# First addends of the gate weights' sums moved from GpSimd's transfers to SyncE's queue, in a two-layer encoder trunk

## The chip, the cores and the metric

One core of one Trainium2 chip runs the whole program. The metric is the device time of one execution in microseconds (us); lower is better. The engines are named as in the profile: PE (TensorE's matmuls), PEld (its weight loads), ACT (ScalarE), DVE (VectorE), POOL (GpSimd), SP (SyncE, which here only issues transfers).

## The reference

```python
def reference(x, p, norm_g, na_w_in, na_rpb, na_w_out, mla_w_in, ..., ple_norm, ple_w_gate, ple_w_proj, final_norm):
    for i in range(DEPTH):                       # two layers
        xn = rmsnorm(x, norm_g[i])
        if i % N_MIXERS == 0:
            y = mixer_na(xn, ...)                # 2-D neighbourhood attention, 16 heads of 64
        else:
            y = mixer_mla(xn, ...)               # latent attention, dense
        h = x + y
        gate = jax.nn.sigmoid(rmsnorm(h, ple_norm[i]) @ ple_w_gate[i])
        x = h + gate * (p[i] @ ple_w_proj[i])
    return rmsnorm(x, final_norm)
```

512 tokens, model width 1024, all in float32. The change concerns `ple_w_gate[i]`, the 1024 x 1024 gate weights of each layer, and the stage of layer 0 in which their sums are made: the neighbourhood attention.

## The kernel before

Every float32 matmul is done as three products of a high part and a remainder (names with `hi`/`lo`, `h`/`l`). A weight tile is loaded by SP into one of three raw buffers (`wraw`), ACT copies its high part (`wwhi`, line 100), POOL subtracts for the remainder (`wwlo`, line 101), and PE multiplies (line 123).

The product with the gate weights is done with seven block products in place of eight (`gate_seven`, both layers). Three of the seven take a quarter of the weights as it is (`quarter` 1, 2 and 3), four take sums of quarters ("f" is the fourth quarter): sum 7 is f + 3, sum 6 is 1 + sum 7, sum 4 is 2 + sum 6, sum 5 is 1 + f. These sums are not made by an engine but by transfers from DRAM to DRAM of 1 MB each: the first addend is copied to its place, the second is added by a transfer that accumulates. Per layer that is eight transfers, 16 in all. In `sum_step` (lines 726 to 730) all 16 are issued by POOL, one in each of the 16 heads of the neighbourhood attention: layer 0's in heads 0 to 7, layer 1's in heads 8 to 15 (heads are counted from 0, two to each j).

A head (`na_head`) is a chain over four engines: score products on PE (`ps_S`, lines 558 and 559), bias and row minimum on DVE (line 568), exponential on ACT (line 576), reciprocal on DVE (line 578), scaling of the rows on POOL (`ex`, line 582), transposes on PE (`ps_T`, lines 594 and 596), copy and remainder on ACT and DVE (`ph`, `pl`, lines 110 and 112), output products on PE (`ps_O`, line 608). `attend` issues a sum's transfer after a head's last scaling on POOL:

```python
with self.tc.issue_after(self.last_norm.ins):
    also(e)
```

While a head's chain runs, PE works on the projections of later heads (`project`, weights `na_qk`), on the late gates (`na_z`) and, at the end of the stage, on the output projection (`na_o`). The order of the instructions on each engine is not written out: the framework's scheduler plays the program through on a simulated timeline and puts an instruction on its engine where it would be ready. So a transfer that is issued elsewhere can change the order on every engine. On the chip each engine takes its instructions strictly in that order. SP's queue carries all loads of the stage: the heads' biases (`bias`, line 540, three buffers), and the weights (`wraw`, line 99).

The sums are loaded as weights by `gate_seven`, those of layer 0 from 258 us on, those of layer 1 near the end of the program.

Of the kernel before, what the change touches and what calls it, by code (L numbers as in the profile page):

```python
# [16 lines left out]
ALU = mybir.AluOpType  # L17
# [12 lines left out]
NLATE = 3  # L30
NEARLY = 7
SEVEN = (0, 1)


def win(t, r0, r1, off, dims):
# [21 lines left out]
class Trunk:  # L57
# [348 lines left out]
    def na_heads(self, pool, xT, zs, Q, xk, weights, more):  # L406
# [73 lines left out]
        def project(j):  # L480
            wq = self.load_w(a["na_qk"][j], 1024)
            psq = self.psum("mm")
            self.proj_T(psq, wq, xT)
            q = queries(psq)
            wk = self.load_w(a["na_qk"][8 + j], 1024)
            psk = self.psum("mm")
            last = self.proj_T(psk, wk, xT)
            k = keys(j, psk)
            key_rests(psk, *k)
            A[j] = (q, edges(q, self.last_key), *k)  # L490
            return last

        def attend(j, also):
            sq, s0, dk, kl = A.pop(j)
            O = []
            for e in range(2):
                c = (2 * j + e) % 4 * P
                O.append(self.na_head(hpool, 2 * j + e, sq[e], s0[e], dk[e], kl[e],
                                      [vt[:, c:c + P] for vt in V[j // 2]]))
                with self.tc.issue_after(self.last_norm.ins):  # L500
                    also(e)
            U[j] = self.combine(hpool, O[0], O[1], 2 + NLATE)
            if j in zs:
                self.gated(U[j], zs[j], oT, j)
# [15 lines left out]
        V = [[Q[kt // 2, g // 2][:, kt % 2 * 2 + g % 2, :] for kt in range(NT)] for g in range(4)]  # L520
        oT = ([self.bigtile(f"oh{g}") for g in range(2)], [self.bigtile(f"ol{g}") for g in range(2)])
        with self.tc.tile_pool(name="nah", bufs=2, reuse_waits="tile") as hpool:
            for j in range(8):
                if 0 < j < 7:
                    last = project(j + 1)
                l, step = divmod(j, 4)
                if step == 0:
                    self.quarters(l)
                attend(j, lambda e: self.sum_step(l, 2 * step + e))
            late = range(8 - NLATE, 8)  # L530
            zs.update(self.z_phase(a["na_z"], xT, late, self.last_exp.ins))
            for j in late:
                self.gated(U[j], zs[j], oT, j)
# [189 lines left out]
        q = lambda n, c: self.a["gate"][layer, n, c:c + 2].rearrange("c p n -> (c p) n")  # L723
        self.quarter[layer] = {1: q(0, 0), 2: q(0, 2), 3: q(1, 2), "f": q(1, 0)}

    def sum_step(self, layer, i):

        p, src, add = ((7, "f", 0), (6, 1, 0), (7, 3, 1), (4, 2, 0), (6, 7, 1), (5, 1, 0), (4, 6, 1), (5, "f", 1))[i]
        src = self.sums[layer][src] if src in (6, 7) else self.quarter[layer][src]
        self.nc.gpsimd.dma_start(self.sums[layer][p], src, accum_op=ALU.add if add else ALU.bypass, max_dma_last_dim=1024)  # L730

    def temp(self, name):
        return self.zp.tile([P, S], F32, name=name, tag="z")
# [437 lines left out]
    def run(self):  # L1171
# [72 lines left out]
        for layer in range(2):  # L1244
            with tc.tile_pool(name=f"out{layer}", bufs=4, reuse_waits="tile") as pool:
                seven = layer in SEVEN
                self.wx, self.wxn = pool, 10 if seven else 5
# [227 lines left out]
```

## Time and profile before

| | before |
|---|---|
| median of 3 runs | 652.94 us (652.29 to 653.63) |
| profiled execution | 653.56 us, its span from first to last instruction 651.5 us |
| PE busy | 640.2 us, 98% of the span |
| POOL busy | 408.4 us, 63% |
| ACT, DVE busy | 453.4 us (70%), 427.7 us (66%) |
| POOL's transfers (q0) | 11040 packets, 18.88 MB, 13.6% of the DMA engines' span |
| SP's transfers (q1) | 34608 packets, 87.12 MB, 39.3% |
| heads of the neighbourhood attention | about 113 to 235 us |

Rows of a timeline give start, duration, engine, line, operation and tiles (written <- read), with the idle time of the engine before it and what ended that in brackets. In rows of waits stand who waited for what, the time in total, how often, and the longest. PE's ends are modelled, so the distance between starts of products says more than their durations.

### The profile page before, as it was taken

What the parts mean: (1) busy time and instruction counts of PE and PEld (TensorE: products, weight loads), DVE (VectorE), ACT (ScalarE), POOL (GpSimd) and SP (SyncE); (2) the same over time, 40 slices, a digit from 0 to 9 for tenths busy, and PEclk for the clock granted to TensorE, in tenths of its full rate; (3) what the DMA queues carried; (4) which work ended last, traced back from release to release, by engine and by line L of the source; (5) the groups of instructions that cost most, each with busy time, mean ns of one, the idle gap of its engine ahead of it and who ended that gap; (6) DMA issues with size and microseconds to landing.
All of it is one profiled execution on the core that took longest, in us unless ns stands there. A gap on an engine that the chain in (4) does not pass through costs nothing.

```text
span 651.5 us, 9980 instructions
## 1 busy us (share of the span) xinstructions
PE 640.2 (98%) x3299; PEld 541.9 (83%) x3299; DVE 427.7 (66%) x886; ACT 453.4 (70%) x903; POOL 408.4 (63%) x371
## 2 busy tenths in 40 slices
PE   9999999999999999999999999999999999999994
PEld 6888878888888888888999887888888888888884
DVE  6197987565665616569715514898988885474665
ACT  7575766887886733788644535897989897547855
POOL 0471006877978853797655516786969887437974
PEclk9999999999999999999999999999999999999997
DMA  9939725778958989446643245120112223683524
GB/s 326 355 124 306 217 66 179 263 205 217 229 209 217 239 178 342 147 154 188 224 140 102 78 109 156 32 75 24 49 50 66 65 84 112 229 292 126 193 65 162
DMA packets 46131, 107.41 MB, mean 165 GB/s; under 512 B 4736, under 2 KB 17792, under 8 KB 46080
## 3 DMA queue, kind: packets, MB, share of 16 engines
q1 hardware_dynamic: 34608, 87.12, 39.3%
q0 software_dynamic: 11040, 18.88, 13.6%
q10 hardware_dynamic: 432, 0.79, 0.3%
q8 instruction: 26, 0.43, 0.3%
q14 instruction: 25, 0.20, 0.1%
HBM read 95.23 MB, written 25.17 MB: 185 GB/s over the span
## 4 chain that ended last, share of the span: by engine, by line
PE 83%; POOL 1%; ACT 1%; DVE 0%; DMA 0%; issue 0%; POOLq 0%
PE ps_mm L123 27%; PE ps_S L123 10%; PE ps_mm L959 7%; PE ps_T L155 6%; PE ps_T L851 5%; PE ps_O L1071 5%; PE ps_mm L851 3%; PE ps_S L851 3%; PE ps_O L608 2%; PE ps_T L123 2%; PE ps_O L123 2%; PE ps_mm L909 2%; PE ps_T L301 2%; PE ps_T L596 2%; PE ps_S L909 1%; PE ps_S L559 1%
## 5 line engine op out<-in xcount | busy, mean ns | idle before, releaser
L101 POOL TENSOR_TENSOR wwlo<-wraw,wwhi 128x1024 fp32r<-128x1024 f32 (+5 forms) x68 | 122.3, 1810 | 93.5 <-ACT wwhi L100 41.9
L796 POOL TENSOR_TENSOR wlo<-wraw,whi 128x512 fp32r<-128x512 f32 x56 | 72.7, 1331 | 22.3 <-ACT whi L794 20.2
L1056 POOL TENSOR_TENSOR ex<-ex,rc 128x512 f32<-128x512 f32 x64 | 66.2, 1043 | 26.6 <-DVE rc L1055 22.5
L100 ACT ACTIVATE wwhi<-wraw 128x1024 fp32r<-128x1024 f32 (+5 forms) x71 | 55.1, 799 | 34.3 <-PE ps_mm L123 18.9
L1054 ACT ACTIVATE ex<-ps_S,mx 128x512 f32<-128x512 f32 x64 | 44.0, 687 | 12.6 <-DVE mx L1052 10.9
L1052 DVE TENSOR_REDUCE mx<-ps_S 128x1 f32<-128x512 f32 x64 | 43.7, 683 | 8.4 <-PE ps_S L123 7.7
L582 POOL TENSOR_TENSOR ex<-ex,rc 128x128 f32<-128x128 f32 (+1 forms) x64 | 37.5, 701 | 17.7 <-DVE rc L578 17.5
L112 DVE TENSOR_TENSOR pt_lo<-ps_T,pt_hi 128x512 fp32r<-128x512 f32 x64 | 43.1, 680 | 7.1 <-ACT pt_hi L110 6.7
L110 ACT ACTIVATE pt_hi<-ps_T 128x512 fp32r<-128x512 f32 x64 | 37.7, 594 | 3.4 <-PE ps_T L155 3.0
L155 PE MATMUL ps_T<-ident,ex 128*128 128x128 f32 x256 | 38.3, 272 | 0.0
L155 PEld LDWEIGHTS ps_T<-ident,ex 128*128 128x128 f32 x256 | 31.5, 140 | 7.5
L123 PE MATMUL ps_mm<-xh,wwhi 128*128 128x512 f32 x120 | 33.7, 404 | 0.0
L221 DVE TENSOR_TENSOR u<-ps_O,u 64x512 f32<-64x512 f32 x32 | 21.9, 685 | 17.7 <-ACT u L220 17.2
L576 ACT ACTIVATE ex<-ex,mx 128x128 f32<-128x128 f32 (+1 forms) x64 | 30.2, 473 | 4.2 <-DVE mx L565 4.1
L123 PE MATMUL ps_mm<-xl,wwhi 128*128 128x512 f32 x120 | 31.9, 395 | 0.0
L794 ACT ACTIVATE whi<-wraw 128x1024 fp32r<-128x1024 f32 x28 | 29.3, 1057 | 3.2 <-DMA wraw<-sum 2.4
L123 PE MATMUL ps_mm<-xh,wwlo 128*128 128x512 f32 x120 | 31.1, 394 | 0.0
L123 PE MATMUL ps_S<-ke,qe 96*128 96x512 f32 x96 | 28.9, 407 | 0.3 <-DMA qe<-rl 0.3
L123 PE MATMUL ps_S<-ko,qo 128*128 128x512 f32 x96 | 28.9, 409 | 0.0
L959 PE MATMUL ps_mm<-cT,wwhi 128*128 128x512 f32 x94 | 27.7, 393 | 0.0
L220 ACT ACTIVATE u<-ps_O 64x512 f32<-64x512 f32 x32 | 18.9, 591 | 12.0 <-PE ps_O L608 8.8
L225 POOL TENSOR_TENSOR u<-u,z 128x512 f32<-128x512 f32 x16 | 22.6, 1412 | 7.5 <-DVE u L221 7.5
(488 smaller groups left out, 1915.1 us busy)
## 6 DMA issues: line engine op xcount, KB each, us to landing
sum<-gate POOLq DMA_DIRECT2D x12, 1024.0 KB, 8.2
wraw<-na_qk SPq DMA_DIRECT2D x16, 512.0 KB, 4.9
wraw<-sum SPq DMA_DIRECT2D x16, 512.0 KB, 3.3
pe<-pe SPq DMA_DIRECT2D x31, 256.0 KB, 5.9
wraw<-gate SPq DMA_DIRECT2D x12, 512.0 KB, 3.3
wraw<-na_v SPq DMA_DIRECT2D x10, 512.0 KB, 3.4
sum<-sum POOLq DMA_DIRECT2D x4, 1024.0 KB, 11.1
wraw<-na_o SPq DMA_DIRECT2D x8, 512.0 KB, 4.8
```

The source lines that it names most:

```text
L100: nc.scalar.activation(hi[:, c], raw[:, c], AF.Copy)
L101: f = lambda e, c=c: e.tensor_tensor(out=lo[:, c], in0=raw[:, c], in1=hi[:, c].bitcast(F32), op=ALU.subtract)
L110: self.last_copy = self.act.activation(hi, src, AF.Copy, scale=scale)
L112: self.dve.tensor_tensor(out=lo, in0=src, in1=hi.bitcast(F32), op=ALU.subtract)
L123: last = self.last_mm = nc.tensor.matmul(out, l, r, start=i == 0, stop=i == n - 1)
L155: self.last_mm = self.nc.tensor.transpose(t[:, i * P:(i + 1) * P], b, self.ident)
L796: nc.gpsimd.tensor_tensor(out=lo[:, o], in0=raw[:, o], in1=hi[:, o].bitcast(F32), op=ALU.subtract)
L851: mm = nc.tensor.matmul(ps, l, r, start=j == 0 and p in banks, stop=j == 11 and p in (2, 3, 4), skip_group_check=True)
L959: self.last_mm = nc.tensor.matmul(PS[key], *terms[i], start=i == 0, stop=i == len(terms) - 1)
L1052: nc.vector.reduce_max(mx, sp, axis=AX.X, negate=True)
L1054: nc.scalar.activation(ex, sp, AF.Exp, bias=mx, accum_out=sm)
L1056: nc.gpsimd.tensor_tensor(out=ex, in0=ex, in1=rc.to_broadcast([P, S]), op=ALU.mult)
```

## The change

The eight plain copies of first addends are issued by SP, the eight additions stay with POOL. The steps are spread anew: `SUMS` gives the head at which each layer's steps begin. For layer 0 the copies stand in heads 2, 3, 4 and 6 and the additions in 4, 5, 6 and 8; for layer 1 in heads 8, 9, 10 and 12, and 10, 11, 12 and 14. The sums and their addends are the same; sum 5 (1, then f) comes earlier in the row of steps.

```diff
+SUMS = (2, 8)
...
+            self.quarters(0)
+            self.quarters(1)
             for j in range(8):
                 if 0 < j < 7:
                     last = project(j + 1)
-                l, step = divmod(j, 4)
-                if step == 0:
-                    self.quarters(l)
-                attend(j, lambda e: self.sum_step(l, 2 * step + e))
+                attend(j, lambda e: self.sum_step(2 * j + e))
...
-    def sum_step(self, layer, i):
-
-        p, src, add = ((7, "f", 0), (6, 1, 0), (7, 3, 1), (4, 2, 0), (6, 7, 1), (5, 1, 0), (4, 6, 1), (5, "f", 1))[i]
-        src = self.sums[layer][src] if src in (6, 7) else self.quarter[layer][src]
-        self.nc.gpsimd.dma_start(self.sums[layer][p], src, accum_op=ALU.add if add else ALU.bypass, max_dma_last_dim=1024)
+    def sum_step(self, i):
+
+        steps = {0: (7, "f"), 1: (5, 1), 2: (6, 1), 4: (4, 2)}, {2: (7, 3), 3: (5, "f"), 4: (6, 7), 6: (4, 6)}
+        for layer in range(2):
+            k = i - SUMS[layer]
+            if k in steps[0]:
+                p, src = steps[0][k]
+                with self.tc.issue_after(self.last_bias.ins):
+                    self.nc.sync.dma_start(self.sums[layer][p], self.quarter[layer][src])
+            if k in steps[1]:
+                p, src = steps[1][k]
+                src = self.sums[layer][src] if src in (6, 7) else self.quarter[layer][src]
+                self.nc.gpsimd.dma_start(self.sums[layer][p], src, accum_op=ALU.add, max_dma_last_dim=1024)
```

In the rows below a line number is that of the kernel in question (the new one's are higher by one, later by eight, for the same statement), and a name's number tells tiles apart; `sum07` is sum 7 of layer 0, `sum16` sum 6 of layer 1.

SP's queue from the first head's bias on, before:

```order
L540 DMA bias_1007<-na_bias 128x384
L540 DMA bias_1065<-na_bias 128x384
L540 DMA bias_1211<-na_bias 128x384
L540 DMA bias_1269<-na_bias 128x384
L99 DMA wraw_1539<-na_qk 128x1024
L540 DMA bias_1415<-na_bias 128x384
L99 DMA wraw_1576<-na_qk 128x1024
L99 DMA wraw_1743<-na_qk 128x1024
L540 DMA bias_1473<-na_bias 128x384
L99 DMA wraw_1780<-na_qk 128x1024
```

The same stretch of SP's queue now:

```order
L540 DMA bias_1007<-na_bias 128x384
L540 DMA bias_1064<-na_bias 128x384
L540 DMA bias_1209<-na_bias 128x384
L734 DMA sum07_101<-gate 16x16384
L540 DMA bias_1267<-na_bias 128x384
L734 DMA sum05_99<-gate 16x16384
L100 DMA wraw_1538<-na_qk 128x1024
L540 DMA bias_1413<-na_bias 128x384
L734 DMA sum06_100<-gate 16x16384
L100 DMA wraw_1575<-na_qk 128x1024
L100 DMA wraw_1742<-na_qk 128x1024
L540 DMA bias_1472<-na_bias 128x384
```

The loads keep their order; three copies of sums now stand among them, two of them ahead of the first weight load after the biases, the third ahead of the next.

PE behind the last score product of head 14 (the first row, `ps_S`), before:

```order
L559 MATMUL ps_S_2368<-la1_512,sa_2179 128x256
L123 MATMUL ps_mm_2509<-xh1_159,wwlo_2505 128x512 x2
L608 MATMUL ps_O_2276<-ph_2263,Q01_680 128x192
L594 MATMUL ps_T_2317<-ident_71,ex_2288 128x2x64
L123 MATMUL ps_mm_2509<-xh1_159,wwlo_2505 128x512 x2
L608 MATMUL ps_O_2276<-pl_2264,Q01_680 128x192
L608 MATMUL ps_O_2276<-ph_2263,Q11_503 128x192
L608 MATMUL ps_O_2276<-pl_2264,Q11_503 128x192
L608 MATMUL ps_O_2276<-ph_2272,Q01_680 128x256
L608 MATMUL ps_O_2276<-pl_2273,Q01_680 128x256
L608 MATMUL ps_O_2276<-ph_2272,Q11_503 128x256
L608 MATMUL ps_O_2276<-pl_2273,Q11_503 128x256
```

PE behind the same score product now:

```order
L559 MATMUL ps_S_2369<-la1_512,sa_2180 128x256
L124 MATMUL ps_mm_2509<-xh1_159,wwhi_2504 128x512 x3
L124 MATMUL ps_mm_2509<-xl0_160,wwhi_2504 128x512 x4
L124 MATMUL ps_mm_2509<-xl1_161,wwhi_2504 128x512 x4
L124 MATMUL ps_mm_2509<-xh0_158,wwlo_2505 128x512 x2
L608 MATMUL ps_O_2277<-ph_2264,Q01_680 128x192
L124 MATMUL ps_mm_2509<-xh0_158,wwlo_2505 128x512 x2
L124 MATMUL ps_mm_2509<-xh1_159,wwlo_2505 128x512
L608 MATMUL ps_O_2277<-pl_2265,Q01_680 128x192
L608 MATMUL ps_O_2277<-ph_2264,Q11_503 128x192
L608 MATMUL ps_O_2277<-pl_2265,Q11_503 128x192
L608 MATMUL ps_O_2277<-ph_2273,Q01_680 128x256
```

Before, four products of the last `na_z` projection (`ps_mm`) stand behind head 14's scores, then the output of head 12, the transposes of head 13, the scores of head 15, and head 14's transposes, the third of which needs the second half of the scaled rows. Now sixteen of these products stand there, and then output products, transposes and scores in nearly the same number.

POOL at the end of the heads, from the addition to sum 6 of layer 1 behind head 12, before:

```order
L730 DMA sum16_104<-sum17_105 1024x256
L101 TENSOR_TENSOR wwlo_2600<-wraw_2598,wwhi_2599 128x1024
L582 TENSOR_TENSOR ex_2288<-ex_2288,rc_2291 128x128
L582 TENSOR_TENSOR ex_2288<-ex_2288,rc_2291 128x256 x3
L730 DMA sum15_103<-gate 1024x256
L582 TENSOR_TENSOR ex_2351<-ex_2351,rc_2354 128x128
L582 TENSOR_TENSOR ex_2351<-ex_2351,rc_2354 128x256 x3
L730 DMA sum14_102<-sum16_104 1024x256
L582 TENSOR_TENSOR ex_2409<-ex_2409,rc_2412 128x128
L582 TENSOR_TENSOR ex_2409<-ex_2409,rc_2412 128x256 x3
L730 DMA sum15_103<-gate 1024x256
L225 TENSOR_TENSOR u_2143<-u_2143,z_2501 128x512
```

The same place on POOL now:

```order
L738 DMA sum16_104<-sum17_105 1024x256
L582 TENSOR_TENSOR ex_2290<-ex_2290,rc_2293 128x128
L582 TENSOR_TENSOR ex_2290<-ex_2290,rc_2293 128x256
L102 TENSOR_TENSOR wwlo_2600<-wraw_2598,wwhi_2599 128x1024
L582 TENSOR_TENSOR ex_2290<-ex_2290,rc_2293 128x256 x2
L582 TENSOR_TENSOR ex_2352<-ex_2352,rc_2355 128x128
L582 TENSOR_TENSOR ex_2352<-ex_2352,rc_2355 128x256 x3
L738 DMA sum14_102<-sum16_104 1024x256
L226 TENSOR_TENSOR u_2144<-u_2144,z_2501 128x512
L582 TENSOR_TENSOR ex_2410<-ex_2410,rc_2413 128x128
L582 TENSOR_TENSOR ex_2410<-ex_2410,rc_2413 128x256 x3
```

The two transfers of sum 5 are gone from between the scalings of heads 13, 14 and 15, the last addition (sum 4, which reads sum 6) still follows head 14's scaling, and a gating product (`u`) now stands between it and head 15's.

## The prediction

> **What bounds the kernel now.** I read the page first, then the waits of PE, then the stage in which the changed transfers run (the neighbourhood-attention heads, 113 to 235 us), and last the rows around the one place where PE waits there.
>
> ```profile
> PE 640.2 (98%) x3299; PEld 541.9 (83%) x3299; DVE 427.7 (66%) x886; ACT 453.4 (70%) x903; POOL 408.4 (63%) x371
> PEclk9999999999999999999999999999999999999997
> ```
>
> PE is busy 98% of the span at a full granted clock. Its ends are modelled, so the share alone proves little; the waits do more.
>
> ```profile
> PE ps_T L301 <- ACT s L51: 1.2, 1, 1.2
> PE ps_T L1187 <- PEq L1464: 0.8, 1, 0.8
> PE ps_T L596 <- POOL ex L582: 0.3, 1, 0.3
> PE ps_S L123 <- DMA qe<-rl: 0.3, 1, 0.3
> ```
>
> Four waits, 2.6 us in all. Only the third lies among the heads. The two rows below are the stretch 113 to 235 us and the largest group of products in it.
>
> ```profile
> 113.00:235.00 122.00, 121.67 (x704) 105.93 (x703) 72.63 (x240) 95.79 (x234) 98.44 (x105) 1.00 0.88 223
> L123 PE MATMUL ps_mm<-xh,wwhi 128*128 128x512 f32 x112 | 31.7, 405 | 0.0
> ```
>
> POOL is busy 98.4 of 122 us and the DMA engines 88%: both are loaded, neither is what PE waits for, except once. That place, with the spacing of each kind of product beside it:
>
> ```profile
> 216.98 0.28 PE L559 MATMUL ps_S<-la,sa 128*128 128x256 f32 x1
> ...
> 219.04 0.82 PE L596 MATMUL ps_T<-ident,ex 128*128 128x128 f32 x6
> 219.62 0.36 PE L558 MATMUL ps_S<-db,s 128*128 128x256 f32 x1
> ...
> 219.94 0.28 PE L558 MATMUL ps_S<-db,sb 128*128 128x256 f32 x1
> 220.06 0.28 PE L559 MATMUL ps_S<-lb,sb 128*128 128x256 f32 x1
> ...
> 220.79 0.33 PE L608 MATMUL ps_O<-ph,Q 128*128 128x192 f32 x1
> 221.45 0.33 PE L596 MATMUL ps_T<-ident,ex 128*128 128x128 f32 x1 [0.33 <-POOL ex L582]
> ...
> 221.71 0.27 PE L608 MATMUL ps_O<-ph,Q 128*128 128x192 f32 x1
> 221.82 0.27 PE L608 MATMUL ps_O<-pl,Q 128*128 128x192 f32 x1
> ...
> 228.36 0.27 PE L594 MATMUL ps_T<-ident,ex 128*128 128x128 f32 x1
> ...
> 230.99 2.00 PE L123 MATMUL ps_mm<-xl,wwhi 128*128 128x512 f32 x8
> 232.82 0.39 PE L123 MATMUL ps_mm<-xh,wwlo 128*128 128x512 f32 x1
> ```
>
> From start to start a 512-wide product takes (232.82 - 230.99)/8 = 0.229 us, a transpose (219.62 - 219.04)/6 = 0.097, a score product 0.12, an output product 0.11. The transpose at 221.45 follows the product at 220.79 by 0.66 instead of 0.11: PE lost 0.55 us there. It belongs to head 14 (heads are counted from 0), whose last score product ended at 216.98 + 0.28 = 217.26, and it waited for this:
>
> ```profile
> 208.03 2.12 POOL L582 TENSOR_TENSOR ex<-ex,rc 128x128 f32<-128x128 f32 x4 [2.31 <-DVE rc L578]
> 210.08 1.29 POOL L730 DMA_DIRECT2D sum<-sum  x1
> ...
> 218.30 3.10 POOL L582 TENSOR_TENSOR ex<-ex,rc 128x128 f32<-128x128 f32 x4 [1.75 <-DVE rc L578]
> 221.67 1.31 POOL L730 DMA_DIRECT2D sum<-sum  x1 [0.28 <-issue]
> ...
> 230.89 1.30 POOL L225 TENSOR_TENSOR u<-u,z 128x512 f32<-128x512 f32 x1
> ```
>
> POOL scaled head 14 from 218.30 to 221.40, after 1.75 us of idleness: it waited for VectorE, not for its own transfers. So from last score product to scaled row took 221.40 - 217.26 = 4.14 us, and PE had less than that to do in between.
>
> **The change, part by part.**
>
> *Eight plain transfers leave GpSimd.* Of the 16 transfers that it issues for the sums, the eight without addition go.
>
> ```profile
> L730 POOL DMA_DIRECT2D sum<-gate x12: 774/1276/1655, 113.6 to 226.2; - x12
> L730 POOL DMA_DIRECT2D sum<-sum x4: 1293/1311/1336, 144.2 to 221.7; - x4
> ```
>
> They are among the twelve of the first row: 8 x 0.774 to 8 x 1.655 gives 6.2 to 13.2 us of POOL time, 10.2 by the median. What PE can get from it is at most the one wait on POOL, 0.55 us, and at least nothing; since POOL was idle just before that wait, I take nothing.
>
> *The order around heads 13 and 14.* Behind head 14's last score product the old order holds four 512-wide products before its third transpose, the new order sixteen. The rest between them is nearly the same (old: 9 output, 9 transpose, 8 score products; new: 8, 7, 8). Old: 4 x 0.229 + 9 x 0.11 + 9 x 0.097 + 8 x 0.12 = 3.7 us, short of the 4.14 that the chain takes, hence the stall. New: 16 x 0.229 + 8 x 0.11 + 7 x 0.097 + 8 x 0.12 = 6.2 us, 2.1 more than the chain. The stall goes: -0.55 us. Bounds: nothing, if another chain comes up short by the same amount, and -0.55. I take -0.55, because the counts give two microseconds to spare. What is late next there is head 13's output: after its transposes come a copy on ScalarE (0.58 us, shown below) and a remainder on VectorE,
>
> ```profile
> L112 DVE TENSOR_TENSOR pl<-ps_T,ph x5: 540/686/691, 214.7 to 224.2; 128x512 fp32r<-128x512 f32 x3, 128x384 fp32r<-128x384 f32 x2
> ```
>
> 0.69 us, together 1.3, and the new order has 7 transposes, 8 score products and three 512-wide ones ahead of it, 2.3 us.
>
> *The same eight on SP's queue.* Each costs SP one issue (0.33 us, row below), and nothing on SP is scarce. What counts is what stands behind them. The first two stand one bias load apart and straight ahead of a weight load that was issued at 109.49.
>
> ```profile
> 102.97 6.43 SPq L540 DMA_DIRECT2D bias<-na_bias  x4
> 109.49 1.67 SPq L99 DMA_DIRECT2D wraw<-na_qk  x1
> ...
> 112.81 7.32 SPq L99 DMA_DIRECT2D wraw<-na_qk  x2
> ```
> ```profile
> wraw<-na_qk SPq DMA_DIRECT2D x1, 512.0 KB, 4.6
> ```
> ```profile
> DMA to landing us min/median/max: 3.2/5.2/7.5
> ```
> ```profile
> W<-na_v SPq DMA_DIRECT2D x2, 1024.0 KB, 7.9
> W<-na_v POOLq DMA_DIRECT2D x2, 1024.0 KB, 14.5
> ...
> sum<-sum POOLq DMA_DIRECT2D x4, 1024.0 KB, 11.1
> ```
> ```profile
> 117.89 1.06 ACT L100 ACTIVATE wwhi<-wraw 128x1024 fp32r<-128x1024 f32 x1
> 118.86 0.58 ACT L110 ACTIVATE ph<-ps_T 128x512 fp32r<-128x512 f32 x1
> ...
> 126.97 1.05 ACT L100 ACTIVATE wwhi<-wraw 128x1024 fp32r<-128x1024 f32 x1
> ```
>
> The first row of the second answer is that one load: it landed 4.6 us after its issue, at 114.1, and ScalarE split it at 117.89, so 3.8 us are to spare. The slowest weight load of the stage took 7.5 us, with GpSimd's transfers in flight beside it; with that it lands at 117.0, still in time. Bounds: nothing at one end; at the other the two transfers one after the other at the 7.9 us of a 1 MB load on this queue. Three biases go out from 102.97 on at 0.33 us each, so the first transfer starts at about 104.0 and lands by 111.9, the second by 119.8, the load by 124.4: 6.5 us late. I take nothing, by the nearer row: those 7.5 us are for loads that already share the DMA engines with these very bytes. The next weight load went out at 112.81 and is split only at 126.97, so it has more to spare.
>
> [...]
>
> *New waits.* GpSimd's additions now wait for SP's plain transfers; two heads lie between them, about 16 us where some 15 heads share 122, and 14.5 us is the slowest MB seen: nothing. The last addition (sum 4 of layer 1) waits for the one before it (sum 6), issued after head 12's scaling at about 210.1 as now; the median of such additions is 11.1 us, so it lands at 221.2, while head 14's scaling ends earlier than before. GpSimd may idle 2 to 4 us there. Queued behind it are a gating product and head 15's scaling; the second rival prices that. Taken: nothing.
>
> **Sum.** -0.55 us from the stall, nothing else on PE's path. The profiled execution took 653.56 us (span 651.5 and 2.06 around it), 0.62 above the median of the three runs; it would come to 653.0, and the median 652.94 to 652.4.
>
> **Rivals.**
>
> *Slower, by SP's queue.* At the serial bound the split at 117.89 runs 6.5 us late, and ScalarE, which works in order, delays the copy at 118.86 by as much. PE first needs that copy here:
>
> ```profile
> 122.17 0.37 PE L608 MATMUL ps_O<-ph,Q 128*128 128x256 f32 x1
> ```
>
> The copy ends at 119.44 and VectorE's remainder 0.69 later, so 2.0 us are to spare. It decides from a load that lands after 119.9, and at the bound the price is 4.5 us: 657.4. For it: two MB straight ahead of the load. Against it: 5.8 us between its landing before and that point.
>
> *Slower, by GpSimd's wait.* After sum 6 lands GpSimd still has to issue sum 4 (1.31), do the gating product (1.30, the last of the POOL rows above) and scale head 15 (2.12), 4.7 us in all, before head 15's transposes, which start at 228.36 now. So it decides from a landing after 223.7, 13.6 us after the issue; beyond it each microsecond costs one. At the 14.5 of the slowest MB on this queue it costs 0.9, at double the usual 11.1 it lands at 232.3 and costs 8.6: 661.5. For it: the wait is sure to be there. Against it: all four such additions have a median of 11.1.
>
> *Faster than can be told from no change.* The 704 matmuls of the stage are 360 512-wide products, 112 transposes, 112 score and 120 output products: 360 x 0.229 + 112 x 0.097 + 112 x 0.12 + 120 x 0.11 = 119.9 of 122 us. If the lighter POOL and DMA engines gave all of the other 2.1 us back, the time would be 650.8. Against it: only 0.55 of it stands at a wait; the rest is in gaps too short to be listed and in the rounding of the spacings.
>
> **How the numbers follow.** What a measurement here can tell from no change is about 0.2%, 1.3 us. The forecast (652.4, within it) gets 0.70; the faster rival 0.16, since it must win nearly everything that PE has left; SP's queue 0.08, GpSimd's wait 0.04, and 0.02 for a new stall that no row points to. So faster 0.16, same 0.70, slower 0.14. The range runs from 651.2 (most of the faster rival, or the scatter of 0.65 us below the median that the runs show, on top of -0.55 and some) to 654.2 (that scatter above, and a new stall or two of 0.55).
>
> **What would show it.** Right: no wait of PE on POOL around 220 us; eight issues of sums with 1 MB each under SP and eight under POOL; POOL's busy time 6 to 13 us down; landings of weight loads in the stage at or below 7.5 us; PE's busy time nearly unchanged. Wrong: PE waiting for an output product's copy near 121 us with ScalarE idle on a weight load; or head 15's transposes waiting for GpSimd, with an idle gap of more than 4 us ahead of the last sum; or a time under 651, with PE's spacing below 0.229.

## The result

| kernel | median, us | range, us | runs |
|---|---|---|---|
| before | 653.03 | 652.29 to 653.63 | 6 |
| after | 658.25 | 657.13 to 659.48 | 6 |

The ratio is 1.008, with a 95% interval of 1.0066 to 1.0094. The change costs 5.2 us where 652.4 was forecast with a range up to 654.2. The profiled execution of the changed kernel took 657.47 us (span 655.7), 0.78 below its median.

The waits of PE in the changed kernel, which answer to the four rows shown for before. Behind the colon: us in total, times, longest.

```profile
PE ps_T L594 <- POOL ex L582: 4.0, 1, 4.0
PE ps_T L302 <- ACT s L52: 1.0, 1, 1.0
PE ps_T L1195 <- PEq L1472: 0.8, 1, 0.8
PE ps_mm L673 <- ACT whi L652: 0.6, 1, 0.6
```

The old wait on GpSimd near 221 us (0.3 in the list) is gone, and a single new one of 4.0 us stands in its place. The page's slices show where, in the slice from 180 to 197 us. This is the one place where PE and its granted clock fall below 9 tenths in the body of the kernel.

```profile
PE   9999999999989999999999999999999999999994
...
PEclk9999999999989999999999999999999999999998
```

GpSimd's rows there, in order of time (start, us, operation, and in brackets its idle time and what ended it):

```profile
160.60 1.28 POOL L738 DMA_DIRECT2D sum<-sum  x1
...
174.11 1.19 POOL L582 TENSOR_TENSOR ex<-ex,rc 128x256 f32<-128x256 f32 x2 [0.17 <-DVE rc L578]
181.53 1.33 POOL L738 DMA_DIRECT2D sum<-sum  x1 [6.22 <-DMA sum<-sum]
182.33 1.52 POOL L582 TENSOR_TENSOR ex<-ex,rc 128x128 f32<-128x128 f32 x2
```

The addition of 160.60 is sum 6 of layer 0, and the one of 181.53 is sum 4, which reads sum 6. GpSimd stood still for 6.22 us until sum 6 had landed. The next head's scaling (182.33) was queued behind the waiting issue, and PE needed that scaling for its transposes:

```profile
178.62 0.71 PE L124 MATMUL ps_mm<-xh,wwhi 128*128 128x512 f32 x2
183.33 0.33 PE L594 MATMUL ps_T<-ident,ex 128*128 128x128 f32 x1 [3.99 <-POOL ex L582]
183.41 0.94 PE L124 MATMUL ps_mm<-xh,wwhi 128*128 128x512 f32 x3
...
184.22 1.52 PE L124 MATMUL ps_mm<-xh,wwhi 128*128 128x512 f32 x3
185.55 3.03 PE L124 MATMUL ps_mm<-xl,wwhi 128*128 128x512 f32 x8
188.41 1.98 PE L124 MATMUL ps_mm<-xh,wwlo 128*128 128x512 f32 x8
190.22 0.28 PE L558 MATMUL ps_S<-da,s 128*128 128x256 f32 x1
```

There is a second loss behind the wait. From 184.22 to 188.41 PE makes 11 products in 4.19 us; at the usual 0.229 they take 2.52. That is 1.67 more. The windows of one microsecond give the reason (the column after the POOL count is PE's granted clock):

```profile
184.00:185.00 1.00, 1.00 (x5) 0.81 (x4) 0.00 (x0) 0.00 (x0) 1.00 (x1) 0.67 1.19 148
185.00:186.00 1.00, 1.00 (x4) 0.71 (x4) 0.00 (x0) 0.00 (x0) 1.00 (x2) 0.50 1.12 162
186.00:187.00 1.00, 1.00 (x4) 0.81 (x3) 0.00 (x0) 0.00 (x0) 1.00 (x4) 0.50 1.20 183
187.00:188.00 1.00, 1.00 (x5) 0.76 (x4) 0.00 (x0) 0.00 (x0) 1.00 (x2) 0.62 1.21 193
```

In windows of 0.1 to 2 us around the edges the clock is 1.00 up to 184.3, 0.50 from 184.4 to 187.7 and 1.00 from 187.8 on. With these two values alone, a clock of 0.67 means that 0.66 of that microsecond ran at half speed, and 0.62 that 0.76 did: 0.66 + 1 + 1 + 0.76 = 3.42 us at half the clock, just after PE had been idle.

The waiting of 3.99 and the 1.67 of slow products, less the 0.55 us of the stall that went, make 5.1 us, where the medians differ by 5.2. That these are so close is partly chance: `e4_l1_late` below has the same order on PE without the wait, and it is 1.2 us faster than the kernel before, not 0.55. Its trace is the better measure. The stretch from 178.62 to 190.22 takes 11.60 us here, and 5.80 there for the same instructions. The difference, 5.80, is nearly all of the 6.1 us between the two spans (655.7 and 649.6), and the wait and the slow products are 5.66 of it.

What made sum 6 late is in the rows of DMA issues (KB each, median us from issue to landing), each taken in a narrow stretch around one issue. Sum 6 of layer 0 in the kernel before took:

```profile
sum<-sum POOLq DMA_DIRECT2D x1, 1024.0 KB, 11.4
```

In the kernel after, the three additions issued at 143.77 (sum 7), 149.04 (sum 5) and 160.60 (sum 6) took:

```profile
sum<-gate POOLq DMA_DIRECT2D x1, 1024.0 KB, 15.1
sum<-gate POOLq DMA_DIRECT2D x1, 1024.0 KB, 24.8
sum<-sum POOLq DMA_DIRECT2D x1, 1024.0 KB, 20.5
```

Two things in the new order meet there. First, sums 7, 5 and 6 now stand on three successive heads, where sum 5 used to come last. Secondly, the copies of layer 1, which the steps put at heads 8, 9 and 10, were issued beside them:

```profile
145.91 0.49 SPq L734 DMA_DIRECT2D sum<-gate  x1
156.31 1.12 SPq L734 DMA_DIRECT2D sum<-gate  x1
162.06 0.49 SPq L734 DMA_DIRECT2D sum<-gate  x1
```

They are ordered behind the bias load of their head (`issue_after(self.last_bias.ins)`), and SP issues the bias loads some heads ahead: the first copy of head 8 left at 145.91, although GpSimd reaches head 8's step only near 175 where nothing holds it up. A copy on SP's queue therefore goes out with that prefetch, some heads ahead of the step that it is written in. GpSimd's transfers stayed where its arithmetic put them.

### The profile page after: what moved, and what is told of

Its sections match the earlier page's. It is cut to its first block, busy times and chain, and to the rows that moved or that the text cites. A ratio compares the mean times of both kernels' runs of the same rounds, so it can differ in the third digit from the quotient of the medians.

```text
span 655.7 us, 9973 instructions
## 1 busy us (share of the span) xinstructions
PE 640.6 (98%) x3299; PEld 542.7 (83%) x3299; DVE 427.2 (65%) x886; ACT 455.3 (69%) x903; POOL 402.3 (61%) x363
## 4 chain that ended last, share of the span: by engine, by line
PE 82%; issue 1%; ACT 1%; POOL 1%; DVE 1%; POOLq 0%
PE ps_mm L124 26%; PE ps_S L124 10%; PE ps_mm L967 7%; PE ps_T L156 6%; PE ps_T L859 5%; PE ps_O L1079 5%; PE ps_mm L859 3%; PE ps_S L859 3%; PE ps_O L608 2%; PE ps_T L124 2%; PE ps_O L124 2%; PE ps_mm L917 2%; PE ps_T L302 2%; PE ps_T L596 1%; PE ps_S L917 1%
## 5 line engine op out<-in xcount | busy, mean ns | idle before, releaser
L582 POOL TENSOR_TENSOR ex<-ex,rc 128x128 f32<-128x128 f32 (+1 forms) x64 | 37.8, 708 | 17.1 <-DVE rc L578 17.1
L111 ACT ACTIVATE pt_hi<-ps_T 128x512 fp32r<-128x512 f32 x64 | 37.8, 595 | 3.3 <-PE ps_T L156 3.0
L222 DVE TENSOR_TENSOR u<-ps_O,u 64x512 f32<-64x512 f32 x32 | 21.9, 685 | 16.1 <-ACT u L221 15.4
L124 PE MATMUL ps_mm<-xh,wwlo 128*128 128x512 f32 x120 | 31.3, 394 | 0.0
L565 DVE CUSTOM_DVE_ANT_0 ex<-ps_S,bias 64x128 f32<-64x128 f32 x32 | 9.2, 288 | 28.4 <-issue 21.0
## 6 DMA issues: line engine op xcount, KB each, us to landing
sum<-sum POOLq DMA_DIRECT2D x4, 1024.0 KB, 11.4
```

Source lines behind the costliest of these rows:

```text
L111: self.last_copy = self.act.activation(hi, src, AF.Copy, scale=scale)
L124: last = self.last_mm = nc.tensor.matmul(out, l, r, start=i == 0, stop=i == n - 1)
```

## The experiments

Theory A: the loss is one late landing, sum 6 of layer 0, and what waits behind it in order: sum 4 on GpSimd, the next head's scaling, PE. Theory B: the traffic of the plain copies costs by itself, through the queue or the memory, wherever it stands. The ratios below are to the kernel before, timed beside each run, with 95% intervals; its medians were 653.09, 653.03 and 652.86 us.

**The last addition one head later** (`e1_last_late`), in both layers.

```
-  {2: (7, 3), 3: (5, "f"), 4: (6, 7), 6: (4, 6)}
+  {2: (7, 3), 3: (5, "f"), 4: (6, 7), 7: (4, 6)}
```

> Edit: the last addition of each layer (sum 4 += sum 6) is issued one head later (layer 0 behind head 9, layer 1 behind head 15); all else as in the changed kernel. Theory A (GpSimd, which works in order, stands at this addition until sum 6 has landed at 181.1, and head 9's scaling stands behind it): the addition is asked for after head 9's scaling, so PE's wait of 4.0 us and the half-clock stretch behind it go; 652 to 653.5 us, 5 us faster than the changed kernel. Rival B (the copies on SP's queue slow the loads or the heads in general): 657 to 659, nothing gained. Rival C (the new order of the heads on PE is what costs): the order of heads 9 to 14 stays as in the changed kernel, so 657 to 659.

Measured: 652.65 us, ratio 1.0007 (0.998 to 1.0034). The transfers are as late as in the changed kernel: sum 6, issued at 161.04, took

```profile
sum<-sum POOLq DMA_DIRECT2D x1, 1024.0 KB, 20.1
```

but sum 4 now stands behind the next head's scaling, and PE's waits hold nothing on GpSimd:

```profile
PE ps_T L302 <- ACT s L52: 1.7, 1, 1.7
PE ps_T L1195 <- PEq L1472: 0.8, 1, 0.8
PE ps_mm L673 <- ACT whi L652: 0.3, 1, 0.3
```

The same late landing, with nobody waiting for it, costs nothing against the kernel before. That is theory A. The runs scatter, however, from 651.3 to 660.3, and the longest had the lowest mean clock (0.990, others 0.994 to 0.997); the traced one is among the short ones, so what waited in the others was not seen.

**Layer 1's copies two heads later** (`e4_l1_late`). PE's instructions have the same order as in the changed kernel.

```
-            if k in steps[0]:
-                p, src = steps[0][k]
+            if k - 2 * layer in steps[0]:
+                p, src = steps[0][k - 2 * layer]
```

> Edit: layer 1's copies are issued two heads later (at steps 10, 11, 12 and 14 in place of 8, 9, 10 and 12), which keeps two of the three copies that run between 146 and 172 us out of layer 0's additions; PE's order is the same as the changed kernel's. Theory A1 (the additions are late because layer 1's copies, pulled about three heads ahead with the bias loads, use the same DMA engines at that time, 2.5 us of each engine for a copy): sum 6 lands about 5 us earlier, at 175 to 177, the wait of GpSimd at sum 4 falls from 6.2 to 0 to 1.5 us, and the time to 652 to 654. Theory A2 (three additions one head apart are too dense by themselves, 6.9 us of every engine each): sum 6 still lands after 179, the wait stays over 4 us and the time at 656 to 659. Rival C (PE's order): 657 to 659.

Measured: 651.84 us (651.36 to 652.41), ratio 0.9978 (0.9969 to 0.9988). It beats both kernels, so the new order on PE is not what costs. Sum 6 landed 13.2 us after its issue, and sum 4 was issued without a wait:

```profile
173.71 1.19 POOL L582 TENSOR_TENSOR ex<-ex,rc 128x256 f32<-128x256 f32 x2 [0.18 <-DVE rc L578]
174.84 1.31 POOL L738 DMA_DIRECT2D sum<-sum  x1
```

PE goes through the stretch in which the changed kernel waits without a stop:

```profile
178.22 0.71 PE L124 MATMUL ps_mm<-xh,wwhi 128*128 128x512 f32 x2
...
184.02 0.28 PE L558 MATMUL ps_S<-da,s 128*128 128x256 f32 x1
```

**All copies in rows of 1 KB** (`e6_small`). The order is again that of the changed kernel, early copies included; only the size of the copies' packets changes.

```
-  self.nc.sync.dma_start(self.sums[layer][p], self.quarter[layer][src])
+  self.nc.sync.dma_start(self.sums[layer][p], self.quarter[layer][src], max_dma_last_dim=1024)
```

> Edit: the copies on SP's queue in rows of 1 KB in place of 64 KB (1024 x 256 in place of 16 x 16384), same places, same PE order as the changed kernel. Theory B1 (an addition's 1 KB packets take turns with a copy's 64 KB packets, which hold a DMA engine for 2.4 us and more at a time, so that the additions starve): the additions land several us sooner, GpSimd's wait of 6.2 us shrinks to under 2, 652 to 654. Theory A (what counts is the engines' time in all and the number of transfers in the stretch): the additions land as late or later, 657 to 660.

Measured: 652.24 us, ratio 0.9986 (0.9977 to 0.9996). The three additions on GpSimd's queue took

```profile
sum<-gate POOLq DMA_DIRECT2D x1, 1024.0 KB, 12.4
sum<-gate POOLq DMA_DIRECT2D x1, 1024.0 KB, 17.1
sum<-sum POOLq DMA_DIRECT2D x1, 1024.0 KB, 15.4
```

and GpSimd waited little, PE not at all:

```profile
176.97 1.33 POOL L738 DMA_DIRECT2D sum<-sum  x1 [1.13 <-DMA sum<-sum]
```

So with the same bytes at the same place in the order, smaller packets on one queue let the other queue's sum 6 land 5.1 us sooner after its issue (15.4 against 20.5). The packet records fit this. In those of the changed kernel a plain copy is 16 packets of 64 KB, each with an engine for 2.4 to 3.8 us, while an addition is 1024 packets of 1 KB at 0.10 us. In rows of 1 KB the copy's packets take about 0.05 us (in `e6_small` the 234 packets of SP's queue that start between 167 and 169 us, 0.24 MB, took 43.8% of 16 engines' 2 us, 0.06 for each). That the additions' small packets wait behind the large ones on each engine is argued from these figures; no view shows one packet waiting for another. The copies pay for it: the one issued in the same stretch landed after 17.0 us instead of 9.7.

**The queue undone, the new spread kept** (`e2_pool_copies`).

```
-  with self.tc.issue_after(self.last_bias.ins):
-      self.nc.sync.dma_start(self.sums[layer][p], self.quarter[layer][src])
+  self.nc.gpsimd.dma_start(self.sums[layer][p], self.quarter[layer][src], accum_op=ALU.bypass, max_dma_last_dim=1024)
```

> Edit: the copies go back to GpSimd's queue, in the new places (steps) of the change; so the queue is undone and the spread stays. Theory A (the spread is at fault: three additions on neighbouring heads, and the last one asked for two heads after the one it reads): GpSimd again waits for a sum's landing, 3 to 6 us, unless the scheduler's order leaves more room; 655 to 659. Rival B (SP's queue is at fault): no wait, 652 to 653.5.

Measured: 655.38 us (654.23 to 660.12), ratio 1.0044 (1.0024 to 1.0063). GpSimd waits for additions here too:

```profile
POOL sum L738 <- DMA sum<-sum: 11.6, 2, 8.3
```

The traced execution is the shortest of the ten, and PE's wait on GpSimd in it is only 0.2 us; where the others lose their time was not seen. The order on PE differs from that of both kernels, too. So the times show that this kernel is slower than the one before; that it is the spread by itself that costs, and how, is only argued.

**The new queue alone, with the old steps** (`e3_sp_old_steps`), an edit of the kernel before.

```
-        self.nc.gpsimd.dma_start(self.sums[layer][p], src, accum_op=ALU.add if add else ALU.bypass, max_dma_last_dim=1024)
+        if add:
+            self.nc.gpsimd.dma_start(self.sums[layer][p], src, accum_op=ALU.add, max_dma_last_dim=1024)
+            return
+        with self.tc.issue_after(self.last_bias.ins):
+            self.nc.sync.dma_start(self.sums[layer][p], src)
```

> Queue alone: the eight plain copies go to SP's queue, while the old steps stay (layer 1's sums behind all of layer 0's; two, not three, additions on successive heads). Theory A (the cost is one late landing, sum 6 of layer 0, behind which GpSimd waits): the additions have two heads each, no wait of PE on GpSimd beyond some tenths of a us, 652.0 to 653.5. Theory B (plain copies on SP's queue cost by themselves, wherever they stand): 655 or more, with PE waits spread over the heads.

Measured: 652.72 us, ratio 1.0001 (0.9991 to 1.0011). PE's waits are those of before, the old one near 221 us included. Together with the run before, this divides the change, though roughly, as the order on PE is a different one in each. The queue with the old steps costs nothing, the new spread on the old queue 2.3 us, both together 5.2.

**The old order of the additions** (`e5_old_adds`): sum 5 last again, layer 1's copies still early.

```
-  {2: (7, 3), 3: (5, "f"), 4: (6, 7), 6: (4, 6)}
+  {2: (7, 3), 4: (6, 7), 6: (4, 6), 7: (5, "f")}
```

> The changed kernel with the old order of the additions: sum 5 goes last instead of between sum 7 and sum 6, so one addition less stands ahead of sum 6 on GpSimd's queue. If the three additions on successive heads are part of the cause, sum 6 lands some 7 us (one addition's share of an engine) sooner, at about 174 instead of 181, the wait of PE goes, and the time is 652 to 653.5. If layer 1's early copies alone are the cause, sum 6 is still late by 5 us or more and the time stays above 655. PE's order differs a little from the changed kernel's, so half a us either way tells nothing.

Measured: 653.56 us, ratio 1.002 (1.0006 to 1.0034). Sum 6, issued at 161.21, took

```profile
sum<-sum POOLq DMA_DIRECT2D x1, 1024.0 KB, 13.1
```

so it landed at 174.3, as expected, and sum 4 was issued at 175.02 without a wait. Either of the two alone, the third addition in a row or the early copies, can be borne; the changed kernel has both. The time is a few hundredths over what was expected. Its order on PE differs, and the stall of 0.55 us near 221 us is back:

```profile
PE ps_T L596 <- POOL ex L582: 0.3, 1, 0.3
```

**Both partial remedies** (`e7_both`): the two edits of `e4_l1_late` and `e6_small` together.

> Layer 1's copies two heads later and all copies in rows of 1 KB: both partial remedies together, PE's order as in the changed kernel. If the transfers are off PE's path once sum 6 lands by about 175, nothing more is to be had: 651.8, as with the later copies alone (651.5 to 652.3). If DMA load still costs PE something small, it gets under 651.3.

Measured: 651.78 us, ratio 0.9984 (0.9975 to 0.9994), as with the later copies alone. Once sum 6 is in time, faster transfers give nothing more.

**Sum 6 made slow on purpose** (`e8_fine`). The edit of `e4_l1_late` stands, and to it comes:

```
-  ... accum_op=ALU.add, max_dma_last_dim=1024)
+  ... accum_op=ALU.add, max_dma_last_dim=512 if (layer, p) == (0, 6) else 1024)
```

> Layer 1's copies two heads later, as in the fastest kernel so far, and only sum 6 of layer 0 is made slow on purpose, by packets of 512 B instead of 1 KB (twice as many for the same bytes). An engine then needs some 13 instead of 6.9 us for it, so it should land at about 179 to 181. Theory A (any late landing of sum 6 costs, whatever makes it late): GpSimd waits 3 to 6 us ahead of sum 4, PE 1.5 to 4 us on GpSimd near 181, then products at half the clock for some us if PE idled long enough, and 654 to 658. Rival (the cost in the changed kernel came from the copies' traffic as such): no change from 651.8.

Measured: 653.09 us (651.9 to 660.81), ratio 1.0018 (0.9989 to 1.0047). The timing alone is unclear; the trace is not. Sum 6 landed 17.5 us after its issue, with

```profile
178.22 1.32 POOL L738 DMA_DIRECT2D sum<-sum  x1 [2.64 <-DMA sum<-sum]
```
```profile
PE ps_T L594 <- POOL ex L582: 0.9, 1, 0.9
```

and no half clock after it: the eight products from 181.68 to 183.53 take 0.231 us each. I had the size wrong. A 512-byte packet took 0.065 us against 0.102 for 1 KB, so an engine needs 8.3 us for the addition instead of 6.5, not twice as much (`e9_fine2` below agrees: 517 packets of 512 B start on GpSimd's queue between 167 and 169 us, which is 16 x 2 / 517 = 0.062 us of an engine for each). The rival, that only the copies' traffic matters, does not explain why PE waits at this very place when two of the three early copies are out of the way, as they are in `e4_l1_late`, where it does not wait.

**Sums 5 and 6 both slow** (`e9_fine2`), the last run with one more transfer in small packets:

```
-  ... max_dma_last_dim=512 if (layer, p) == (0, 6) else 1024)
+  ... max_dma_last_dim=512 if (layer, p) in ((0, 5), (0, 6)) else 1024)
```

> Layer 1's copies two heads later, and now sums 5 and 6 of layer 0 both in packets of 512 B: twice the added load ahead of sum 4. One fine addition made sum 6 land 4.5 us later (177.9 against 173.3) and PE wait 0.9 us; two should bring it to about 182 to 185. Theory A (PE waits one microsecond for each by which sum 4 is issued after about 177.3, whatever makes sum 6 late): a wait of 4.5 to 8 us on GpSimd, then some 3 us at half the granted clock as in the changed kernel, and 657 to 662. Rival (the changed kernel's loss, and its half clock, belong to the copies' traffic): the wait comes but the clock stays at 1.0 after it, or the time stays under 655.

Measured: 653.23 us, ratio 1.0002 (0.9991 to 1.0013). The expectation missed: GpSimd waited 2.63 us ahead of sum 6's own issue instead,

```profile
163.79 1.86 POOL L738 DMA_DIRECT2D sum<-sum  x1 [2.63 <-PE ps_O L608]
```

sum 6 then landed only 12.9 us later, and there was no wait at sum 4. The named releaser is hardly what ended the wait, since this transfer reads nothing of PE's. Sum 7, which it does read, had landed at 155.3. Sum 5 landed at 163.5, just ahead of the issue; whether the issue waited for that transfer, which it does not read, and why it should, was not settled. GpSimd's pause cost PE about a microsecond by another way. ScalarE waited 3.48 us for a gating product of GpSimd (`u`), VectorE then 3.93 us for ScalarE, and the next scaling came late. From the transpose at 177.36 to the products at 182.44 PE took 5.08 us, against 4.12 for the same instructions in `e4_l1_late` (176.26 to 180.38). The run says nothing on a long wait without the copies.

**The changed kernel once more** (`e10_again`), on the chip of the last run.

> The changed kernel once more, nothing altered, beside the last one and on its chip. If the loss is a fixed collision of transfers, sum 4 of layer 0 is again issued at 181 to 182 after a wait on sum 6, PE waits 3.5 to 4.5 us there, products run at half the clock for some 3 us after it, and the time is 657 to 659.5. If it was an accident of the first profile, wait or clock differ.

Measured: 658.11 us, ratio 1.0082 (1.0067 to 1.0097). Sum 6 landed 20.1 us after its issue, sum 4 went out at 180.96, and PE waited again:

```profile
PE ps_T L594 <- POOL ex L582: 3.6, 1, 3.6
```

The collision is fixed, not an accident. The half clock is there again, but longer:

```profile
181.00:182.00 1.00, 0.00 (x0) 0.00 (x0) 0.97 (x2) 0.38 (x1) 1.00 (x2) 0.88 0.00 0
182.00:183.00 1.00, 0.23 (x2) 0.24 (x2) 0.20 (x1) 0.00 (x0) 1.00 (x4) 0.50 0.01 0
...
187.00:188.00 1.00, 1.00 (x4) 0.71 (x3) 0.00 (x0) 0.01 (x1) 0.95 (x1) 0.50 1.24 199
188.00:189.00 1.00, 1.00 (x5) 0.82 (x4) 0.00 (x0) 0.61 (x1) 0.31 (x1) 0.71 1.22 209
```

The rows left out have a clock of 0.50; windows of 0.2 us show 0.50 from 181.8 on, still 0.50 from 188.2 to 188.4, and 1.00 from 188.6. So it is 0.24 + 6 + 0.58 = 6.8 us, the first of these microseconds while PE was still idle. The products behind the wait are slow for longer, too:

```profile
182.77 0.47 PE L594 MATMUL ps_T<-ident,ex 128*128 128x128 f32 x1 [3.57 <-POOL ex L582]
182.89 1.63 PE L124 MATMUL ps_mm<-xh,wwhi 128*128 128x512 f32 x3
184.32 0.41 PE L596 MATMUL ps_T<-ident,ex 128*128 128x128 f32 x1
184.38 1.63 PE L124 MATMUL ps_mm<-xh,wwhi 128*128 128x512 f32 x3
185.81 3.29 PE L124 MATMUL ps_mm<-xl,wwhi 128*128 128x512 f32 x8
188.93 1.98 PE L124 MATMUL ps_mm<-xh,wwlo 128*128 128x512 f32 x8
```

Four traces with one and the same order on PE give the price of lateness. Counted from sum 7's issue, sum 4 goes out after 174.84 - 143.54 = 31.3 us in `e4_l1_late` (PE waits 0), 178.22 - 143.52 = 34.7 in `e8_fine` (0.93), 180.96 - 143.64 = 37.3 in `e10_again` (3.57) and 181.53 - 143.77 = 37.8 in the changed kernel (3.99). From 34.7 on, 2.6 us more cost 2.64 and 3.1 more cost 3.06: each microsecond costs one, from 33.8 on. Three more traces have this order. In `e6_small` and `e7_both` sum 4 goes out after 32.0 and 30.7 us and PE does not wait; in `e9_fine2` it goes out after 34.7, but there the scaling ahead of it was late already, so it is left out of the rule.

## Why the prediction was wrong

*The step that failed* is "New waits", taken at nothing. The mechanism was on record as the second rival: GpSimd waits for the addition before the last, and a scaling is queued behind it. I priced it for layer 1 alone, where the last addition stands at head 14. There GpSimd did wait and PE did not, as forecast. I did not put the same question to layer 0, where the same pair of additions stands two heads apart and deeper in traffic.

*The term that was mis-sized* is the landing of such an addition. I took the median of 11.1 us and the slowest MB seen, 14.5, from a kernel in which no three additions stood on successive heads and no 64 KB packets of sums ran beside them. In the changed kernel it was 20.5, and 24.8 for the one ahead of it. With the threshold above, layer 0's sum 4 could go out until 143.77 + 33.8, about 177.5. It went out 0.4 us after sum 6 had landed (181.1), so sum 6, issued at 160.60, had some 16.5 us to land without cost. Had I asked the question at this place with 14.5 us, the answer would still have been "no cost"; only with the load on the queue counted does it turn. I weighed the sharing of the DMA engines for the weight load on SP's queue alone (7.5 us at the slowest before), not for the additions on GpSimd's queue, whose landings were the ones that cost time (sum 6 of layer 0: 11.4 us before, 20.5 after).

*The price per microsecond* was right for the wait and incomplete behind it: 1.67 us of products at half the clock were in no term. Both slower rivals were also priced from the median of 652.94, without the stall's -0.55; from the forecast they come to 656.9 and 661.0.

*Eight transfers leave GpSimd*: held. POOL's busy time fell from 408.4 to

```profile
PE 640.6 (98%) x3299; PEld 542.7 (83%) x3299; DVE 427.2 (65%) x886; ACT 455.3 (69%) x903; POOL 402.3 (61%) x363
```

402.3, by 6.1 us, just under the lower end of the 6.2 to 13.2; it was worth nothing to PE, as taken.

*The stall near 221 us*: held. The three runs with PE's old order around heads 13 and 14 or near it (before, `e3_sp_old_steps`, `e5_old_adds`) list that wait; the other runs do not (where they wait on GpSimd, it is at 179 to 183 us). `e4_l1_late` shows about what the change would have brought without the collision: 651.84, 1.2 us below before in the medians, of which 0.55 is this stall and the rest lies in small differences ahead of and behind the heads that I did not take apart.

*SP's queue*: held. The load behind the two copies was issued at 109.79 and landed after 6.6 us, at 116.4, and its split ran at 117.60; no wait of PE stands near 121 us, and the queue with the old steps (`e3_sp_old_steps`) costs nothing. Two of the figures were off without a cost: the slowest weight load of the stage took 10.8 us to land, not the 7.5 that the prediction gave as a sign of being right, and the issue of a copy took SP 0.49 to 1.12 us, not 0.33. ScalarE's waits among the heads hold none on a load.

## What to carry to other kernels

When transfers are moved or spread anew, list for each wait that an in-order engine makes on a landing what stands on the same queue ahead of that transfer, and what the other queues issue meanwhile, at every place where the pattern occurs and not only at the last. The median landing of the kernel before (11.1 us here) is no bound for the new order (20.5). An issue tied to a prefetch goes out when the prefetch does, here at 145.91 us, where the step that it is written in comes near 175; and a wait that an engine need not make yet belongs behind its urgent work, which here took nearly the whole loss away (652.65 us in `e1_last_late`, 658.25 in the changed kernel).

## What the runs showed of the hardware

The half clock after an idle PE lasted 3.42 us in the first trace of the changed kernel and 6.8, twice as much, in the second, with waits of 3.99 and 3.57 us; with the wait of 0.93 in `e8_fine` the products behind it kept their 0.231 us. The clock fell at 185 - 0.66 = 184.34 in the first trace and at 182 - 0.24 = 181.76 in the second. PE stood from 179.34 to 183.33 and from 179.20 to 182.77 (by its modelled ends), so the clock fell 1.0 us after PE had begun again in the one and 1.0 us before PE began again in the other. What sets the time of the fall, and why nearly equal waits were followed by 3.42 and by 6.8 us of half clock, was not shown. The wait of 3.99 us cost 1.7 us more behind it in the first trace, and that of 3.57 us 2.7 in the second (14 products and a transpose from 182.89 to 188.93, 6.04 us instead of 14 x 0.229 + 0.097 = 3.30), while the one of 0.93 us cost only itself.

The size of one queue's packets changed how soon another queue's transfers landed, at equal bytes. Beside 64 KB packets of one queue the 1 KB additions of the other took 20.5 us for a MB, beside 1 KB packets of the same bytes 15.4.

Lastly, the releaser that a trace names for a waiting issue is not always the right one: in `e10_again` the wait of 5.8 us at sum 4 was put down to VectorE, though sum 6 landed 0.4 us ahead of the issue, and the first trace of the changed kernel names that transfer for the same wait.
